# Experts' weights in 2 MB transfers with 16 KB pieces, model columns in another order, and two steps of the norms moved

## The chip, the cores and the metric

The kernel runs on one core of one Trainium2 chip. The metric is the device time of one execution in microseconds; lower is better. Three runs of the kernel before took 1532.81, 1531.54 and 1533.71 us (median 1532.81).

## What is computed

A hybrid encoder of two layers on 256 tokens of 1024 columns, all in float32. Cut to what matters here:

```python
h = layer_norm(x, emb_ln_g, emb_ln_b)
for l in range(2):
    mix = token_mixing(h, ...)                    # four branches, gates, w_branch, w_out
    h = layer_norm(ALPHA * h + mix, ln1_g[l], ln1_b[l])
    ffn = hierarchical_moe(h, ...)                # 32 experts, two per token
    h = layer_norm(ALPHA * h + ffn, ln2_g[l], ln2_b[l])

z = hs @ w_in                                     # 1024 x 8192, split among branches and gates
y_a, y_b, y_c, y_d = ...                          # 2-D window, differential, pooling, dilated
gates = sigmoid(z_gate + b_gate)
merged = sum(gates[n] * (y[n] @ w_branch[n]) for n in range(4))
mix = merged @ w_out

ye = (silu(xb @ w_gate[e]) * (xb @ w_up[e])) @ w_down[e]   # 1024 x 512, 1024 x 512, 512 x 1024
```

An expert has 6 MB of weights, a layer's 32 experts 192 MB (MB is 1024 x 1024 bytes where weights and places are counted; the GB/s of the profile are 10^9 bytes).

## The kernel before

**Stages.** A start (norm of x, `run`, L387), and then per layer `mixing` (L451) and `moe` (L796). `mixing` multiplies the normalised, transposed tokens (kept as a high and a low part, `hth` and `htl`) with column blocks of `w_in`, each block split into a high part by ScalarE (`high`, L232) and a low part by VectorE (`low`, L237), three products for one. There are two forms of product: with tokens in rows (`natural`, L465 in the profile) and with columns in rows (`crosswise`, L484). The four attention and pooling branches come first, then the four gated branch projections in `BRANCH_ORDER` (loop at L756), then `w_out`. `moe` begins with `output_and_route` (L1063: product with `w_out`, norm, router, choice of experts, gather of the first four experts' tokens), then `overflow` (L1324, which runs only where an expert has over 64 tokens), then the loop over 32 experts (L925), and a tail that combines the last expert and starts the next layer.

**The order of the work.** `mixing` is put in order by the framework's scheduler, which places each engine's instructions by its own estimate of when they can run. The start, `output_and_route`, the expert loop and the tail are inside `manual_schedule`, where each engine runs the instructions as written. Each engine is in order, and so is SP, which issues the weights' DMAs: a request that waits for a free place holds those behind it.

**The ring.** All weights pass through places in SBUF of 1 MB: 8 in the pool `rawp` (open throughout), 4 in `rawb` (opened before the third gated branch, L757), 5 in `rawc` (opened by `open_ring`, L128, in the step "ring" of `output_and_route`) and 1 in `rawd` (opened at L871, its load requested at L924, as the expert loop starts). `weight_sources` (L146) gives the order of the transfers, `load_weight` (L181) requests the next one into a new tile of a pool, `take` (L223) hands a source's tiles to the user, and its `free` requests the next transfer into the same pool when a tile has been used. So 17 MB of a layer's experts are requested before the stage, and the 18th as it starts. A transfer of `w_in` is 1 MB in pieces of 2 KB.

**An expert's weights.** Gate and up are each two transfers of 1 MB, in the order gate 0, up 0, gate 1, up 1; each has pieces of 8 KB contiguous in HBM and in SBUF (`f p k`: half, partition, four rows). Down is two transfers of 1 MB (8 KB pieces) and comes behind the next expert's pair. The very last down is two column halves, eight transfers of 256 KB with 1 KB pieces ("halves"). The model columns therefore stand in the order (f p k), in the gathered tokens too (`nat`, `xh`, `xl`: `j=4` in `bk`, L1156).

**The expert loop.** Expert p has twelve steps. Steps 0 to 7 multiply gate and up of one row block each (`products`, L850; L854 in the profile, two matmuls a step), steps 8 to 11 the down-projection of expert p-1 (`down`, L893). After step 3 gate 0 and up 0 are free, after step 7 gate 1 and up 1, after steps 9 and 11 the halves of down. The steps in `STEPS` (copy of the result `evacuate`, `turn`, `silu`, `combine` and so on) and the gather of later experts stand between. The first four steps of expert 0 (`begin`, L856) run before `overflow`.

**Norms.** `turn_rows` (L311, called at L421 for the first norm, outside `manual_schedule`) transposes the norm's scale and shift on TensorE (L317) and copies them with ScalarE (L318). `enter_mixing` (L331) finds the statistics (`norm_stats`, L258; square root on ScalarE, L272), keeps TensorE busy with `FILL[0]` = 28 small matmuls (`keep_busy`, L352; L356 in the profile), and normalises. `finish_h` (L380, called at L537) loads scale and shift as rows (two broadcasts of 512 KB on SP) and applies them to h with four operations on VectorE (L384, L385); its result is needed only where h is added after `w_out`.

**Small tiles.** `t4` has 6 buffers of 4 KB per partition, `t2` 8 of 2 KB. The slots' selection tiles (`gs`, L812) and the overflow's gathered tokens are in `t4`.

Of the kernel before, what the change touches and what calls it, by code (L numbers as in the profile page):

```python
# [29 lines left out]
FILL = (28, 16)  # L30
G = 2
# [75 lines left out]

class Kernel:
# [19 lines left out]
    def open_ring(self):  # L128

        self.close_side()  # L130
        self.side = [self.tc.tile_pool(name=f"rawc{self.layer}", bufs=RAW[2] * 2 // G + 1, side="right", reuse_waits="tile")]
        self.rawc, = (p.__enter__() for p in self.side)
        for _ in range(RAW[2] * 2 // G + 1):
            self.load_weight(self.rawc)

    def close_side(self):
        for p in self.side[::-1]:
            p.__exit__(None, None, None)
        self.side, self.rawc = [], None
# [6 lines left out]
    def weight_sources(self):  # L146
        a = self.a
        for l in range(self.depth):
# [14 lines left out]
            yield l, [(a["const_big"][:, :2048].rearrange("p (k c) -> p k c", k=4), 512)]  # L163
# [9 lines left out]
            for e in range(N_EXP + 1):  # L173
                if e < N_EXP:
                    yield l, [(a[name][l, e].rearrange("(f p k) c -> p f k c", f=2, k=4), 512)
                              for name in ("expert_w_gate", "expert_w_up")], "pair"
                if e:
                    src = a["expert_w_down"][l, e - 1].rearrange("(h p k) d -> p h k d", h=2, k=2)
                    yield l, [(src, D)], "halves" if e == N_EXP else "down"

    def load_weight(self, pool):  # L181

        nc = self.nc
        if self.ahead is None:
            self.ahead, self.part = next(self.sources, None), 0
        if self.ahead is None or (pool in (self.rawb, self.rawc, self.rawd) and self.ahead[0] > self.layer):
            return
        blocks, kind = (*self.ahead[1:], False)[:2]
        if self.part == 0:
            self.loaded.append([[], 1024 // sum(w for _, w in blocks)])  # L190
        qs, q = self.loaded[-1][0], self.part
        if kind:


            parts = 4 if kind == "pair" else 2
            if kind == "pair":
                t = pool.tile([128, 4, 512], F32, tag="raw", name="raw")
                nc.sync.dma_start(t, blocks[q % 2][0][:, q // 2])
            elif kind == "down":
                t = pool.tile([128, 2, 2, 512], F32, tag="raw", name="raw")  # L200
                nc.sync.dma_start(t.rearrange("p k f c -> p k (f c)"), blocks[0][0][:, q])
            else:
                t = pool.tile([128, 4, 2, 256], F32, tag="raw", name="raw")
                src = blocks[0][0].rearrange("p h k (f i c) -> p h k f i c", f=2, i=2)
                for k in range(4):
                    nc.sync.dma_start(t[:, k], src[:, k // 2, k % 2, :, q])
            qs.append((t, pool, True))
            self.part += 1
        else:
            width = sum(w for _, w in blocks)  # L210
            r = 1024 // width
            parts = blocks[0][0].shape[1] // r
            t = pool.tile([128, r * G, width], F32, tag="raw", name="raw")
            o = 0
            for src, w in blocks:
                nc.sync.dma_start(t[:, :, o:o + w], src[:, q * r:(q + G) * r])
                o += w
            qs += [(t[:, i * r:i * r + r], pool, i == G - 1) for i in range(G)]
            self.part += G
        if self.part == parts:  # L220
            self.ahead = None

    def take(self):  # L223
# [3 lines left out]
        def free(i):  # L227
            if qs[i][2]:
                self.load_weight(qs[i][1])
# [158 lines left out]
    def run(self):  # L388
        tc, nc, a = self.tc, self.nc, self.a
        with ExitStack() as ctx:  # L390
            pool = lambda name, bufs, **kw: ctx.enter_context(tc.tile_pool(name=name, bufs=bufs, **kw))
            const = pool("const", 1)
            self.rawp = pool("raw", RAW[0] * 4 // G)
            self.rawb = self.rawc = self.rawd = None
# [1035 lines left out]
```

## Time and profile before

| | us |
|---|---|
| median of three runs | 1532.81 |
| the profiled execution | 1530.08 |
| its span in the trace | 1528.0 |
| TensorE busy | 1467.8 (96%) |
| VectorE busy | 571.0 (37%) |
| ScalarE busy | 468.7 (31%) |
| moved by DMA | 501.16 MB, mean 328 GB/s |

The profile is of one execution: busy time of each engine, the span in 40 slices, and a trace of every instruction with what released it. PE is TensorE, PEld its weight load, DVE VectorE, ACT ScalarE, SP SyncE. The clock is the share of full speed that TensorE was granted. A bracket behind a timeline row tells how long the engine stood idle before it and what ended that. An fp32 matmul leaves two records. Layer 0's expert loop ends near 755 us, layer 1 begins behind it.

### The profile page before, as it was taken

The page shows a single profiled execution, that of the slowest core. Times are in us where ns is not written, and L with a number is a line of the kernel's source. Part 1 is how long each engine was busy: PE and PEld are TensorE (multiplying, and loading weights), DVE is VectorE, ACT ScalarE, POOL GpSimd, SP SyncE. Part 2 cuts the span into 40 slices and gives each one's busy share as a digit, 9 for nine tenths or more (in the row PEclk, how much of TensorE's full clock was granted, in tenths as well). Part 3 has the DMA queues.
Part 4 walks back from the last instruction along what each step waited for, and adds up shares of the span by engine and source line. Part 5 has one row for each costly group of instructions (what it writes and reads, how often), then busy time and mean ns, then how long its engine had stood idle before and what let it go on. Part 6 is the DMA issues. An engine that isn't in the chain of part 4 may idle for free. (4 is left out here: it accounts for less than half of the span.)

```text
span 1528.0 us, 21590 instructions
## 1 busy us (share of the span) xinstructions
PE 1467.8 (96%) x8848; PEld 896.1 (59%) x8848; DVE 571.0 (37%) x1202; ACT 468.7 (31%) x764; POOL 0.2 (0%) x4
## 2 busy tenths in 40 slices
PE   8989999999999999999899999999999999999995
PEld 7777899844444444444378778997444444444432
DVE  5477765721111111111176766665111111111103
ACT  5445555521111111111264555454111111111111
POOL 0000000000000000000000000000000000000000
PEclk9989999999999999999999999999999999999998
DMA  9744485679999999999988336746999999999996
GB/s 334 230 167 138 136 303 195 249 306 419 420 420 419 420 420 419 419 420 421 391 246 308 111 111 214 252 167 254 395 420 420 419 420 420 419 420 420 421 420 217
DMA packets 121658, 501.16 MB, mean 328 GB/s; under 512 B 23050, under 2 KB 35786, under 8 KB 72660
## 3 DMA queue, kind: packets, MB, share of 16 engines
q1 hardware_dynamic: 121248, 499.14, 83.8%
q8 instruction: 72, 1.18, 0.3%
q10 hardware_dynamic: 308, 0.60, 0.1%
q14 instruction: 30, 0.25, 0.0%
HBM read 498.65 MB, written 2.00 MB: 328 GB/s over the span
## 5 line engine op out<-in xcount | busy, mean ns | idle before, releaser
L854 PE MATMUL bank<-raw,xs 128*64 128x512 f32 x2048 | 481.7, 595 | 20.0 <-DMA raw<-in_expert_w_up_dram 19.9
L854 PEld LDWEIGHTS bank<-raw,xs 128*64 128x64 f32 x2048 | 166.3, 137 | 302.2 <-issue 239.5
L896 PE MATMUL bank<-raw,act 128*64 128x512 f32 (+1 forms) x1056 | 261.0, 586 | 0.0
L239 DVE TENSOR_TENSOR wl<-raw,wh 128x1024 fp32r<-128x1024 f32 x159 | 192.6, 1222 | 113.7 <-ACT wh L234 110.0
L876 ACT COPY hid<-bank 128x512 f32<-128x512 f32 x64 | 68.3, 1067 | 457.9 <-PE bank L854 457.9
L234 ACT CAST wh<-raw 128x1024 fp32r<-128x1024 f32 x159 | 165.6, 1050 | 136.6 <-PE mm L484 60.6
L831 DVE COPY xs<-bank 128x256 f32<-128x256 f32 x116 | 43.9, 420 | 421.9 <-PE bank L822 421.9
L484 PE MATMUL mm<-hth,wh 128*128 128x256 f32 x576 | 162.8, 283 | 0.0
L484 PE MATMUL mm<-hth,wl 128*128 128x256 f32 x576 | 162.4, 282 | 0.0
L484 PE MATMUL mm<-htl,wh 128*128 128x256 f32 x576 | 162.2, 282 | 0.0
L896 PEld LDWEIGHTS bank<-raw,act 128*64 128x64 f32 x1056 | 78.4, 136 | 130.8 <-issue 124.6
L908 DVE SCALAR_TENSOR_TENSOR y<-bank,tg,y 128x512 fp32r<-128x512 f32 (+1 forms) x66 | 48.5, 735 | 178.0 <-ACT y L907 178.0
L484 PEld LDWEIGHTS mm<-hth,wh 128*128 128x128 f32 x576 | 109.1, 189 | 2.4 <-issue 2.2
L484 PEld LDWEIGHTS mm<-htl,wh 128*128 128x128 f32 x576 | 109.2, 190 | 1.1 <-issue 0.8
L484 PEld LDWEIGHTS mm<-hth,wl 128*128 128x128 f32 x576 | 109.1, 189 | 1.0 <-issue 0.8
L907 ACT ACTIVATE y<-bank,tg 128x512 fp32r<-128x512 f32 (+1 forms) x66 | 44.5, 674 | 166.2 <-PE bank L896 166.2
L465 PE MATMUL mm<-wh,hth 128*128 128x512 f32 x220 | 72.7, 402 | 1.0 <-ACT hth L300 1.0
L465 PE MATMUL mm<-wl,hth 128*128 128x512 f32 x220 | 71.7, 401 | 0.0
L465 PE MATMUL mm<-wh,htl 128*128 128x512 f32 x220 | 70.2, 398 | 0.0
L822 PEld LDWEIGHTS bank<-g,xh 128*128 128x128 f32 x240 | 36.9, 192 | 50.9 <-issue 50.9
L888 ACT ACTIVATE act<-bank 128x256 f32<-128x256 f32 x64 | 24.6, 385 | 127.7 <-PE bank L882 125.5
L822 PE MATMUL bank<-g,xh 128*128 128x256 f32 x240 | 55.0, 311 | 3.7 <-DVE g L813 3.7
(228 smaller groups left out, 1453.6 us busy)
## 6 DMA issues: line engine op xcount, KB each, us to landing
raw<-in_expert_w_gate_dram SPq DMA_DIRECT2D x128, 1024.0 KB, 19.9
raw<-in_expert_w_up_dram SPq DMA_DIRECT2D x128, 1024.0 KB, 19.9
raw<-in_expert_w_down_dram SPq DMA_DIRECT2D x124, 1024.0 KB, 19.9
raw<-in_w_in_dram SPq DMA_DIRECT2D x56, 1024.0 KB, 7.7
raw<-in_w_in_dram SPq DMA_DIRECT2D x16, 512.0 KB, 11.1
raw<-in_w_branch_dram SPq DMA_DIRECT2D x8, 1024.0 KB, 6.3
raw<-in_w_out_dram SPq DMA_DIRECT2D x8, 1024.0 KB, 8.1
raw<-in_expert_w_down_dram SPq DMA_DIRECT2D x16, 256.0 KB, 13.8
```

Source lines behind the costliest of these rows:

```text
L234: self.nc.scalar.copy(hi, s)
L239: self.nc.vector.tensor_sub(lo, s, raw(hi))
L465: nc.tensor.matmul(ps[T], s[:, kk, T * 128:(T + 1) * 128], m[:, k], stop=kk == 7 and s is stat[1], start=kk == 0 and s is stat[0] and m is wh)
L484: nc.tensor.matmul(ps[j // 2][:, j % 2], m[:, k, j * 128:(j + 1) * 128], s[:, kk], start=j % 2 == 0 and kk == 0 and m is wh and s is hth, ...
L822: nc.tensor.matmul(ps[:, o:o + 256], (xh, xl)[i][:, T, k], gs[e0][:, T], start=i == 0 and T == 0, stop=i == 1 and T == 1)
L831: (nc.scalar.copy if on_scalar else nc.vector.tensor_copy)(xs[e0 + 2 * i][:, :, 2 * j:2 * j + 2], ps[:, 2 * i:2 * i + 2])
L854: nc.tensor.matmul(gu[half[i]], x, w, start=k == 0, stop=k == 7)
L876: nc.scalar.copy(st["h", e].rearrange("q (h k p) -> q h p k", h=2, k=2), gu.rearrange("q (h p k) -> q h p k", h=2, k=2))
L888: nc.scalar.activation(st["a", e], fv[:, :, 0], AF.Silu)
L896: nc.tensor.matmul(ps[half[f], :w.shape[2]], st["a", e][:, k], w[:, f], start=k == 0, stop=k == 3)
L907: nc.scalar.activation(yh, ps, AF.Copy, scale=g)
L908: nc.vector.scalar_tensor_tensor(yl, ps, g, raw(yh), op0=ALU.mult, op1=ALU.subtract)
```

## The change

An expert's gate, up and down become one transfer of 2 MB each, with 16 KB contiguous per partition: gate, up, then the down of the expert before. The model columns stand in the order (p k), eight consecutive rows to a partition, and the inner columns in (p k) with four. Places are of 2 MB (two units): 4 in `rawp`, 2 in `rawb`, 2 in `rawc`. A place is reloaded when all units in it are freed. An odd MB stays: `rawe` (opened with the ring) takes the first half of expert 3's gate, and `load_loose` its second half, in two `t4` tiles of 512 KB (a new step "loose" in `output_and_route`, behind the last transposes of the tokens); later it is reloaded into `rawe` and `rawd` as two transfers of 1 MB with 8 KB pieces. So 18 MB are requested before the stage, and the request at the start of the expert loop is gone. The mixing weights' transfers are what they were, but two share a place; the constants ("alone") have a place for themselves.

`turn_rows` for the first norm moves into the manual schedule ahead of the statistics, `FILL[0]` goes from 28 to 22, `finish_h` moves from the start of `mixing` to before the last gated branch, and `gs` and the overflow's tokens move from `t4` to `t2`.

```diff
-FILL = (28, 16)
+FILL = (22, 16)
...
     def open_ring(self):
         self.close_side()
-        self.side = [self.tc.tile_pool(name=f"rawc{self.layer}", bufs=RAW[2] * 2 // G + 1, side="right", reuse_waits="tile")]
-        self.rawc, = (p.__enter__() for p in self.side)
-        for _ in range(RAW[2] * 2 // G + 1):
+        self.side = [self.tc.tile_pool(name=f"{n}{self.layer}", bufs=b, side="right", reuse_waits="tile")
+                     for n, b in (("rawc", RAW[2] // G), ("rawe", 1))]
+        self.rawc, self.rawe = (p.__enter__() for p in self.side)
+        for _ in range(RAW[2] // G):
             self.load_weight(self.rawc)
+        self.load_first()
...
-                    yield l, [(a[name][l, e].rearrange("(f p k) c -> p f k c", f=2, k=4), 512)
+                    yield l, [(a[name][l, e].rearrange("(p k) c -> p (k c)", k=8), 512)
                               for name in ("expert_w_gate", "expert_w_up")], "pair"
                 if e:
-                    src = a["expert_w_down"][l, e - 1].rearrange("(h p k) d -> p h k d", h=2, k=2)
+                    src = a["expert_w_down"][l, e - 1].rearrange("(p k) d -> p (k d)", k=4)
...
+    def load_odd(self):
+        if self.peek() and self.ahead[0] == self.layer:
+            self.fill([p.tile([128, 2048], F32, tag="raw", name="raw") for p in (self.rawe, self.rawd)], self.load_odd)
+
+    def load_first(self):
+        self.peek()
+        self.odd = self.fill([self.rawe.tile([128, 2048], F32, tag="raw", name="raw")], self.load_odd)
+
+    def load_loose(self):
+        (_, blocks, kind), q = self.ahead, self.part
+        assert kind == "pair" and q % 2
+        ts = [self.t4.tile([128, 2, 512], F32, tag="t4", name="raw") for _ in range(2)]
+        for i, t in enumerate(ts):
+            o = 2048 * (q % 2) + 1024 * i
+            self.nc.sync.dma_start(t.rearrange("p k c -> p (k c)"), blocks[q // 2][0][:, o:o + 1024])
+        self.loaded[-1][0].append((Two(*ts), self.odd))
+        self.odd[0] += 1
+        self.step(4)
...
+            if kind in ("pair", "down"):
...
+                n = 2 if whole is not None and u == q % 2 == 0 else 1
+                o = q % 2 * 2048
+                nc.sync.dma_start(whole if n == 2 else t, src[:, o:o + 2048 * n])
+                qs += [(r(units[u + i]), place) for i in range(n)]
+                place[0] += n
...
         def free(i):
-            if qs[i][2]:
-                self.load_weight(qs[i][1])
+            place = qs[i][1]
+            place[0] -= 1
+            if place[0] == 0:
+                place[1]()
...
             with tc.manual_schedule():
+                self.turn_rows(rows, 0)
                 for T in range(2):
...
             if l == 0:
                 self.router_weights(l)
-            self.finish_h(*(a["ln2_" + n][l - 1] if l else a["emb_ln_" + n] for n in "gb"))
...
+            if n == BRANCH_ORDER[3]:
+                self.finish_h(*(a["ln2_" + n][l - 1] if l else a["emb_ln_" + n] for n in "gb"))
...
-                    gs[e0] = t4.tile([128, 2, batch, CAP], F32R, tag="t4", name="g")
+                    gs[e0] = t2.tile([128, 2, batch, CAP], F32R, tag="t2", name="g")
...
-                nc.scalar.copy(st["h", e].rearrange("q (h k p) -> q h p k", h=2, k=2),
-                               gu.rearrange("q (h p k) -> q h p k", h=2, k=2))
+                nc.scalar.copy(st["h", e].rearrange("q (k p) -> q p k", k=4), gu.rearrange("q (p k) -> q p k", k=4))
...
             with tc.manual_schedule():
-                self.load_weight(self.rawd)
...
-                            i = s // 4 * 2
+                            i = s // 4
                             if p or s >= 4:
-                                products(p, s, tiles[i][:, s % 4], tiles[i + 1][:, s % 4])
+                                products(p, s, tiles[i][:, s % 4], tiles[i + 2][:, s % 4])
                             if s % 4 == 3:
                                 free(i)
-                                free(i + 1)
+                                free(i + 2)
...
-            nc.scalar.copy(xh[:, T, 4 * f:4 * f + 4], nat[T][f])
+            nc.scalar.copy(xh[:, T, :, 64 * f:64 * f + 64], nat[T][f])
...
-                nat[T] = [at().rearrange("q (j p) -> q j p", j=4) for _ in range(2)]
-            i = k % 4 * 32
-            nc.tensor.transpose(nat[T][k // 4][:, :, i:i + 32].rearrange("q j p -> q p j"), piece(T, k), c["ident"])
+                nat[T] = [at().rearrange("q (j p) -> q j p", j=8) for _ in range(2)]
+            i = k % 4 * 16
+            nc.tensor.transpose(nat[T][k // 4][:, :, i:i + 16].rearrange("q j p -> q p j"), piece(T, k), c["ident"])
...
         bks(1)
+        S("loose", self.load_loose)
```

## Rows read from the trace of the kernel before

**Rows 1.** The page: span, engines, DMA share in 40 slices, one of the issue groups

```profile
span 1528.0 us, 21590 instructions
...
PE 1467.8 (96%) x8848; PEld 896.1 (59%) x8848; DVE 571.0 (37%) x1202; ACT 468.7 (31%) x764; POOL 0.2 (0%) x4
...
DMA  9744485679999999999988336746999999999996
...
raw<-in_expert_w_up_dram SPq DMA_DIRECT2D x128, 1024.0 KB, 19.9
```

**Rows 2.** Windows: us, busy PE PEld DVE ACT POOL (x), clock, DMA share, GB/s

```profile
70.00:75.00 5.00, 5.00 (x23) 4.03 (x22) 1.50 (x2) 0.00 (x0) 0.00 (x0) 1.00 1.04 387
86.00:92.00 6.00, 6.00 (x40) 5.34 (x41) 5.92 (x7) 0.00 (x0) 0.00 (x0) 0.54 0.20 37
313.72:317.00 3.28, 2.13 (x18) 2.00 (x18) 0.50 (x2) 0.65 (x2) 0.00 (x0) 1.00 0.69 215
313.70:333.00 19.30, 18.10 (x123) 9.21 (x124) 2.62 (x8) 3.18 (x5) 0.00 (x0) 1.00 0.94 368
400.00:700.00 300.00, 295.75 (x1620) 132.76 (x1616) 51.51 (x123) 45.59 (x64) 0.00 (x0) 1.00 1.01 420
1062.64:1066.00 3.36, 1.97 (x10) 1.97 (x11) 0.53 (x2) 0.04 (x1) 0.00 (x0) 0.74 0.66 222
1062.60:1082.00 19.40, 17.93 (x114) 9.69 (x116) 2.67 (x8) 2.95 (x5) 0.00 (x0) 0.91 0.84 330
```

**Rows 3.** PE's timeline at starts and ends of stages: start, us, instruction, wait before

```profile
314.87 0.50 PE L822 MATMUL bank<-g,xh 128*128 128x256 f32 x2 [1.75 <-DVE g L813]
...
1064.03 0.61 PE L822 MATMUL bank<-g,xh 128*128 128x256 f32 x2 [1.97 <-DVE g L813]
...
1492.95 3.65 PE L854 MATMUL bank<-raw,xs 128*64 128x512 f32 x16 [0.68 <-DMA raw<-in_expert_w_up_dram]
1497.92 3.22 PE L854 MATMUL bank<-raw,xs 128*64 128x512 f32 x13 [1.31 <-DMA raw<-in_expert_w_up_dram]
```

**Rows 4.** DVE's timeline at layer 0's first softmax

```profile
80.55 2.35 DVE L384 TENSOR_TENSOR h<-h,ln 128x1024 f32<-128x1024 f32 x2
82.82 2.35 DVE L385 TENSOR_TENSOR h<-h,ln 128x1024 f32<-128x1024 f32 x2
85.09 0.21 DVE L619 RECIPROCAL m<-m 128x1 f32<-128x1 f32 x2
```

**Rows 5.** PE's timeline behind the first softmax of layer 0 and of layer 1

```profile
85.82 1.97 PE L623 MATMUL at<-cs,p 128*128 128x128 f32 x8 [6.55 <-DVE p L620]
...
834.34 0.66 PE L623 MATMUL at<-cs,p 128*128 128x128 f32 x4 [0.47 <-DVE p L620]
```

**Rows 6.** ACT's timeline at the start

```profile
12.70 0.17 ACT L318 COPY cols<-mm 128x16 f32<-128x16 f32 x1 [9.95 <-PE mm L317]
12.77 0.48 ACT L272 ACTIVATE w<-mv,eps 128x1 f32<-128x1 f32 x2
```

**Rows 7.** DVE's timeline at the start

```profile
10.12 0.27 DVE L273 TENSOR_SCALAR w<-mv 128x1 f32<-128x1 f32 x2
```

**Rows 8.** PE's timeline at the start

```profile
3.67 8.41 PE L356 MATMUL spare<-cs 128*128 128x128 f32 x48 [3.67 <-DMA cs<-in_const_small_dram]
```

**Rows 9.** ACT's timeline at layer 0's first softmax

```profile
80.77 0.71 ACT L618 ACTIVATE p<-p,m 128x512 f32<-128x512 f32 x1
```

**Rows 10.** SP's timeline: first requests of the experts' stages of both layers

```profile
313.72 0.34 SPq L198 DMA_DIRECT2D raw<-in_expert_w_up_dram  x1
...
321.59 0.80 SPq L201 DMA_DIRECT2D raw<-in_expert_w_down_dram  x2
...
1062.64 0.34 SPq L198 DMA_DIRECT2D raw<-in_expert_w_up_dram  x1
...
1072.21 0.80 SPq L201 DMA_DIRECT2D raw<-in_expert_w_down_dram  x2
```

**Rows 11.** The page's costliest groups: DVE's splits of weights in mixing

```profile
L239 DVE TENSOR_TENSOR wl<-raw,wh 128x1024 fp32r<-128x1024 f32 x159 | 192.6, 1222 | 113.7 <-ACT wh L234 110.0
```

More of the change, by code (lines that the diff above doesn't have):

```diff
@@ L179, in weight_sources, with units @@
                     yield l, [(src, D)], "halves" if e == N_EXP else "down"
+    def units(self, pool):
+        t = pool.tile([128, 2, 2048], F32, tag="raw", name="raw")
+        return t.rearrange("p u c -> p (u c)"), [t[:, 0], t[:, 1]]
     def load_weight(self, pool):
-        nc = self.nc
+        if self.peek() and (pool is self.rawp or self.ahead[0] == self.layer):
+            whole, units = self.units(pool)
+            self.fill(units, lambda: self.load_weight(pool), whole)
+    def load_odd(self):
+        if self.peek() and self.ahead[0] == self.layer:
+            self.fill([p.tile([128, 2048], F32, tag="raw", name="raw") for p in (self.rawe, self.rawd)], self.load_odd)
@@ L184, in load_weight, with peek @@
+    def peek(self):
         if self.ahead is None:
             self.ahead, self.part = next(self.sources, None), 0
[L186 to L219, printed above, removed]
@@ L220, in load_weight, with step, fill @@
+        return self.ahead
+    def step(self, parts, n=1):
+        self.part += n
         if self.part == parts:
             self.ahead = None
+    def fill(self, units, reload, whole=None):
+        nc = self.nc
+        place = [0, reload]
+        u = 0
+        while u < len(units) and self.peek():
+            blocks, kind = (*self.ahead[1:], False)[:2]
+            width = 512 if kind == "pair" else sum(w for _, w in blocks)
+            if self.part == 0:
+                self.loaded.append([[], 1024 // width])
+            qs, q, t = self.loaded[-1][0], self.part, units[u]
+            if kind in ("pair", "down"):
+                src, r = blocks[q // 2][0], (lambda x: x.rearrange("p (k c) -> p k c", k=4)) if kind == "pair" else (
+                    lambda x: x.rearrange("p (k f c) -> p k f c", k=2, f=2))
+                n = 2 if whole is not None and u == q % 2 == 0 else 1
[3 more added lines that the diff above has]
+                place[0] += n
+                self.step(4 if kind == "pair" else 2, n)
+                u += n
+                continue
+            if kind == "halves":
+                t = t.rearrange("p (k f c) -> p k f c", k=4, f=2)
+                src = blocks[0][0].rearrange("p (k f i c) -> p k f i c", k=4, f=2, i=2)
+                for k in range(4):
+                    nc.sync.dma_start(t[:, k], src[:, k, :, q])
+                qs.append((t, place))
+                place[0] += 1
+                self.step(2)
+            else:
+                r = 1024 // width
+                parts = blocks[0][0].shape[1] // r
+                t = t.rearrange("p (k w) -> p k w", w=width)
+                o = 0
+                for src, w in blocks:
+                    nc.sync.dma_start(t[:, :, o:o + w], src[:, q * r:(q + G) * r])
+                    o += w
+                qs += [(t[:, i * r:i * r + r], place) for i in range(G)]
+                place[0] += G
+                self.step(parts, G)
+                if kind == "alone":
+                    u += 1
+            u += 1
+        return place
@@ L861, in begin @@
                 for s in range(4):
[L862 removed]
+                    products(0, s, tiles[0][:, s], tiles[2][:, s])
             gu = ahead = None
```

35 lines of the change are left out of this document (19 added, 16 removed).

## The prediction

> **What bounds the kernel now.** I read the page first, then the windows of steady streaming, then SP's timeline where the experts' stage starts, then the places where PE stands still. The page gives a span of 1528.0 us with PE busy for 96% of it and the DMA engines full in both experts' stages and half idle in both mixing stages [rows 1]. So the kernel has two bounds. In mixing it is PE: weights arrive far ahead. In the experts' stage it is the weight stream. It moves 420 GB/s without a gap from 400 to 700 us [rows 2]; PE needs less than that per expert, so it lives on the 17 MiB loaded before the stage until they are used up, and in the last experts of each layer it waits for weights, at the very end 0.68 and 1.31 us before the two halves of the last expert [rows 3]. The layer then ends a fixed chain of work after the last up-projection has landed. Hence an edit of the stream counts only by how much earlier the last pair is in, and an edit of PE's work counts only in mixing, at the start, or behind that landing.
>
> PE has two real gaps outside: 6.55 us at 79.3, where DVE stands between a softmax and its products [rows 4, 5], and the first microseconds.
>
> **The change, part by part.** Sums are against the profiled execution: 1530.08 us, of which 1528.0 is span. The median of the runs shown is 1532.81, 2.7 more; I carry the difference of the sum over to the median. A measurement of this kernel can tell about 0.2%, 3.1 us.
>
> *A. Start.* ACT's square root runs at 12.77, behind the copy of the turned rows, for which ACT waited 9.95 us because PE had filler matmuls queued ahead of the turn [rows 6]. Its operands were there at about 10.25: DVE's step on the same statistics starts at 10.12, with the aggregate before it [rows 7]. With the turn put ahead of the statistics the copy is done early: -2.5 us. Of the 28 fillers 24 take 8.41 us (48 records, two each), 0.35 us one; 22 take 7.7 and keep PE at work to about 12, close to the first transposes of h [rows 8]. Bounds 0 (if the weights, not h, were last) and -2.5.
>
> *B. finish_h away from layer 0's first softmax.* Its four operations hold DVE from 80.55 to 85.09; the reciprocal that leads to PE's 85.82 stands behind them [rows 4, 5]. Without them it waits for the second exponential, which starts at 80.77 and takes 0.71 [rows 9]: it starts at about 81.4, so -3.7. What is late next is PE's own chain, or nothing: in layer 1, where the same four operations fall into a stretch with PE at work, PE fills the same softmax with crosswise products and stands only 0.47 us [rows 5]. Then 6.1 of the 6.55 us go, and what the clock took goes too: at 86 to 92 it was 0.54, after the stop [rows 2], which costs about 3 us at half speed. That end is -9.4 (6.1 + 3.3). The order of this stage is a scheduler's, so I take the middle, -6.
>
> *C. Stream rate.* A piece of 2 KB takes a DMA engine 2048 B / (387/16 GB/s) = 84.7 ns, one of 8 KB 8192 / (420/16) = 312.1 ns [rows 2]. The straight line through both gives 615.3 ns for 16 KB: 426 GB/s. No row has a 16 KB piece, so bounds: nothing (the pieces cost per byte, or are cut), and 436 GB/s, if the two doublings from 387 to 420 (16.5 GB/s each) are followed by a third as large. I take the line, since it is the form in which a fixed cost per piece would show. A MiB takes 2.497 us at 420 and 2.461 at 426. A layer's 192 MiB less the last down-projection and less the 18 MiB loaded before leave 172 to stream; 8 of 9 of them go in 16 KB pieces (the odd place keeps 8 KB): 153 x 0.0352 = -5.4 us per layer, bounds 0 and -14.0.
>
> [...]
>
> *D. Later resume.* The stream stops with the ring full before the stage. Today it resumes at 313.72 in layer 0 and 1062.64 in layer 1 with the extra place, and half a pair later with the next two [rows 10]. After the change a place of 2 MB comes free only when both halves of gate and up are used, which is where the first down-projections are requested today: 321.59 and 1072.21 [rows 10]. That is +7.9 and +9.6. One MiB more is already in: -2.5. The slow start stays, but its sequel, the queue running dry again between the small early requests, goes, since 4 MB are asked for at once. Lost after the resume today: 19.3 x (1 - 368/420) = 2.4 and 19.4 x (1 - 330/420) = 4.2 us, of which 1.6 in the first 3.3 us [rows 2]; so -0.8 and -2.6 go. Net +4.6 and +4.5; I write +4.5 per layer. In the steady stretch the coarser places cost nothing: PE hands back 6 MB per expert, and several requests are always queued (19.9 us from issue to landing, eight transfers of 2.5 us each [rows 1]). That cover ends only if PE falls behind the stream, which it does not.
>
> *E. Tail.* Today the first half of the last pair is multiplied (16 matmuls, 3.65 us by the profile, 3.4 by their spacing) before the second half is in [rows 3]. With up behind gate in two whole transfers no product can start before the last one: +3.4 per layer. Queued behind it on PE are the down-projection of expert 30, its combine and the last expert's chain, all of which DVE and ACT wait for, so all of it shows.
>
> *F. Clock.* The waits of 0.68 and 1.31 [rows 3] become one of about 2 us. Stops of 1.75 us left the clock at full speed, one of 1.97 did not [rows 3]; the stretch behind that one had 0.91 on average over 19.4 us, 1.7 us lost, against 1.00 in layer 0 [rows 2]. In earlier experts the loss eats slack, in the last it shows: 0 to +1.7, I take +0.7 per layer.
>
> [...]
>
> *G. The rest.* finish_h in the last branch: four DVE operations of 1.2 us; there DVE waits for ACT's casts for 113.7 us in 159 operations [rows 11], so they fit. Their two tiles join h's two and the gates of two branches in the six t4 buffers, so the last branch's first gate can wait on ACT for a tile, and PE behind it for a bank; at most one pass of DVE's four operations per layer: bounds 0 and +10, taken +0.3, since DVE is mostly waiting there. Its two loads of 512 KB on SP stand ahead of experts' reloads in a full ring: 0. Mixing reloads only after both halves of a 2 MB place: up to half a place later, covered by the other three, with DMA at 40 to 80% [rows 1]: 0. The two loose loads wait on SP for t4 tiles, with nothing behind them before the resume: 0. Strided split, transposes and hid copy move the same elements: 0, within 0.5 either way. The slots' tiles in t2: 0.
>
> Sum: -2.5 - 6 + 2 x (-5.4 + 4.5 + 3.4 + 0.7) + 0.3 = -1.8. Profiled 1528.3, median **1531.0**.
>
> **The rivals.** *1, slower: no gain of rate.* For it: nothing shows what a piece above 8 KB does, and the busy share at 8 KB already reads 1.01 [rows 2]. Late resume and tail are then unpaid: C is 0, the sum is +9.0, 1541.8. It decides below 425.0 GB/s (4.5 us per layer, no change), and is seen as slower below 423.3.
>
> *2, faster: more rate and the softmax filled.* At 430 GB/s C is -8.9 per layer: 1524.0; with B at -9.4, 1520.6. For it: layer 1 fills that softmax [rows 5], and 387 to 420 shows that larger pieces help. [...] With the full 436 it would be 1513.8; I give that end 0.05 of this rival's chance.
>
> [...]
>
> *3, the change doesn't do what it says in mixing:* the scheduler puts the softmax's casts where they were and PE still stands, or finish_h lands on another critical softmax: B is 0 to -2, 1535 to 1537.
>
> **How the numbers follow.** The forecast, with terms inside their bounds, has 0.45: 0.15 of it faster by over 0.2% (below 1529.7), 0.27 within, 0.03 slower. Rival 1 has 0.17, slower. Rival 2 has 0.30, faster. Rival 3 has 0.08, half within 0.2%, half slower (above 1535.9). Sum: faster 0.45, same 0.31, slower 0.24. The range goes from a little below rival 2 to rival 1, 1519 to 1542, and leaves out about 0.08 below and 0.1 above; the forecast's own is 1526 to 1536.
>
> **What the profile after would show.** A: the square root near 10.3 and the first product near 14.7. B: the stop of 6.55 us gone or about 3 us, the clock at 1.0 behind it. C: a steady window at 425 to 427 GB/s; 420 is rival 1, 430 or more rival 2. D: the first reload after the eighth product pair, then no window below the steady rate. E: 32 products of the last expert after one wait, ending about 2.5 us later relative to the stage's start. F: the clock in the last expert. G: PE without idle time in the last branch. I am wrong if the rate is outside 423 to 430, or if PE waits for weights in the middle of a stage, which would say that the coarse places starve the stream.

## The result and the profile after

The changed kernel took 1539.5 us (median of five runs, 1538.44 to 1543.71) beside 1532.81 (five runs, 1528.42 to 1533.71): ratio 1.0065, 95% interval 1.004 to 1.0089 (the two medians alone give 1.0044). It is slower by 0.65%, where 1531.0 was forecast; the time lies inside the range of 1519 to 1542, on the wrong side of "no change". The ratios below leave out two executions of one kernel, e13, which took 1825.04 and 4205.61 us.

The profiled execution's span is 1536.4 us, 8.4 more than before [rows 1]. Its page:

```profile
span 1536.4 us, 21199 instructions
...
PE 1473.8 (96%) x8836; PEld 891.4 (58%) x8836; DVE 571.1 (37%) x1202; ACT 468.8 (31%) x764; POOL 0.2 (0%) x4
...
DMA  9733585759999999999976236745999999999994
...
raw<-in_expert_w_up_dram SPq DMA_DIRECT2D x64, 2048.0 KB, 30.6
```

128 transfers of 1 MB have become 64 of 2 MB. The steady window, two stretches behind the first softmax and a stretch in which PE was at half clock (columns as in [rows 2]):

```profile
400.00:700.00 300.00, 295.00 (x1608) 131.36 (x1608) 51.34 (x123) 45.08 (x64) 0.00 (x0) 1.00 1.01 426
...
79.50:83.00 3.50, 3.25 (x14) 2.86 (x15) 3.01 (x6) 3.50 (x4) 0.00 (x0) 0.52 0.05 19
...
86.00:92.00 6.00, 5.72 (x49) 5.03 (x48) 5.48 (x13) 2.46 (x5) 0.00 (x0) 1.00 0.70 229
...
309.70:316.10 6.40, 6.33 (x15) 1.80 (x15) 0.47 (x2) 0.00 (x0) 0.00 (x0) 0.57 0.00 0
```

The stream runs at 426 GB/s after 420, as forecast. At 86 to 92 us the clock is 1.00 where it was 0.54; the half clock is not gone but stands at 79.5 to 83.0, behind the shorter stop. At 309.7, in the middle of the first expert, it is 0.57 and no byte moves. PE's timeline there, in layer 0 and in layer 1:

```profile
304.11 1.07 PE L916 MATMUL bank<-raw,xs 128*64 128x512 f32 x2
309.77 6.31 PE L916 MATMUL bank<-raw,xs 128*64 128x512 f32 x14 [4.59 <-SPq L1404]
316.01 0.50 PE L884 MATMUL bank<-g,xh 128*128 128x256 f32 x2
...
1060.39 1.07 PE L916 MATMUL bank<-raw,xs 128*64 128x512 f32 x2
1065.68 5.34 PE L916 MATMUL bank<-raw,xs 128*64 128x512 f32 x14 [4.22 <-SPq L1404]
1070.95 0.51 PE L884 MATMUL bank<-g,xh 128*128 128x256 f32 x2
```

Before, the 16 records of `begin`'s eight matmuls ran in one piece of 3.65 us (309.46 and 1058.41), followed by a stop of 1.75 or 1.97 and the gather [rows 3]. Now one matmul runs, PE stands for over 4 us, and the other seven follow at a clock of 0.57, in layer 1 of 0.68 (1065.6 to 1071.0). What ends the stop is SP at L1404, the head of `overflow`'s loop (L1342 before). From first product to gather it takes 11.90 and 10.56 us after 5.41 and 5.62.

The tail, PE's timeline behind the last landing of each layer:

```profile
746.93 6.65 PE L916 MATMUL bank<-raw,xs 128*64 128x512 f32 x29 [1.48 <-DMA raw<-in_expert_w_up_dram]
...
757.37 3.66 PE L957 MATMUL bank<-raw,act 128*64 128x512 f32 x24
...
1502.17 6.65 PE L916 MATMUL bank<-raw,xs 128*64 128x512 f32 x29 [1.48 <-DMA raw<-in_expert_w_up_dram]
...
1512.63 3.66 PE L957 MATMUL bank<-raw,act 128*64 128x512 f32 x24
```

The same points before were 747.45 and 754.45, 1497.92 and 1504.94. From them the ledger of the 8.4 us (us, after less before, each between two such points):

| stretch | layer 0 | layer 1 |
|---|---|---|
| start, to the first mixing product (17.18 to 14.96) | -2.2 | |
| mixing, to the first expert product | -3.1 | -1.0 |
| first expert product to the gather behind the loop | **+6.5** | **+4.9** |
| gather to the landing of the last pair | -1.7 | -2.7 |
| landing to the last down-projection | +3.4 | +3.4 |
| rest | 0 | +0.7 |

The third line is more than the whole. The experiments are about it first, and then about the tail, the rate and the norms.

### The profile page after: what moved, and what is told of

Same layout as the page of the kernel before. It is cut to its first block, busy times and chain, and to the rows that moved or that the text cites. A ratio compares the mean times of both kernels' runs of the same rounds, so it can differ in the third digit from the quotient of the medians.

```text
span 1536.4 us, 21199 instructions
## 1 busy us (share of the span) xinstructions
PE 1473.8 (96%) x8836; PEld 891.4 (58%) x8836; DVE 571.1 (37%) x1202; ACT 468.8 (31%) x764; POOL 0.2 (0%) x4
## 3 DMA queue, kind: packets, MB, share of 16 engines
q8 instruction: 72, 1.18, 0.3%
## 5 line engine op out<-in xcount | busy, mean ns | idle before, releaser
L916 PE MATMUL bank<-raw,xs 128*64 128x512 f32 x2048 | 493.3, 599 | 27.9 <-DMA raw<-in_expert_w_up_dram 19.1
L957 PE MATMUL bank<-raw,act 128*64 128x512 f32 (+1 forms) x1056 | 265.7, 586 | 0.0
L957 PEld LDWEIGHTS bank<-raw,act 128*64 128x64 f32 x1056 | 82.8, 136 | 125.4 <-issue 116.0
L952 DVE TENSOR_TENSOR act<-act,bank 128x256 f32<-128x256 f32 x64 | 27.0, 422 | 76.5 <-ACT act L949 71.2
```

What stands on the lines that cost most here:

```text
L916: nc.tensor.matmul(gu[half[i]], x, w, start=k == 0, stop=k == 7)
L952: nc.vector.tensor_mul(st["a", e], st["a", e], fv[:, :, 1])
L957: nc.tensor.matmul(ps[half[f], :w.shape[2]], st["a", e][:, k], w[:, f], start=k == 0, stop=k == 3)
```

## The experiments

### Why PE stands at the loop

Two things in the traces could do it. First, SP stops at the loop's head for loads that are still under way. SP's timeline of after, in which the last 6 MB are requested, and its waits at the loop (us in total, times, longest):

```profile
289.48 0.33 SPq L252 DMA_DIRECT2D raw<-in_expert_w_up_dram  x1
289.95 0.34 SPq L252 DMA_DIRECT2D raw<-in_expert_w_down_dram  x1
290.34 0.42 SPq L252 DMA_DIRECT2D raw<-in_expert_w_gate_dram  x1
290.81 1.83 SPq L221 DMA_DIRECT2D raw<-in_expert_w_gate_dram  x2
322.72 0.34 SPq L252 DMA_DIRECT2D raw<-in_expert_w_up_dram  x1
```
```profile
SPq L1404 <- SPq L1404: 4.0, 3, 1.9
```

These waits are instructions of the program. At that line (`tc.For_i` in the source) SP has 16 semaphore instructions per layer (from the view of line L1404: how many, shortest, median and longest in ns, first and last start):

```profile
L1404 SPq EVENT_SEMAPHORE  x32: 17/17/28, 304.6 to 1065.7; - x32
```

The first eight wait for the eight semaphores on which SP's transfers report (in layer 0 they run from 304.57 to 308.86, before from 310.24 to 310.74). Three of them waited for over 0.15 us in layer 0.

DMA's rate in 40 slices of 0.75 us from 300 us, after and before:

```profile
GB/s 415 371 426 437 355 328 284 371 284 60 44 0 22 0 0 0 0 0 0 0 0 0 0 0 0 0 0 0 0 0 0 262 87 350 371 481 415 393 393 502
```
```profile
GB/s 448 426 437 404 470 393 109 0 0 0 0 0 22 0 0 11 0 0 0 109 120 437 393 437 426 448 404 448 404 426 339 251 404 415 426 448 426 339 229 481
```

Before, the ring was full at 305, ahead of the loop at 313; now the last bytes land at 308, with SP already in it from 305. Second, PE's instructions stand in another order, though neither program line was moved: the scheduler put the loop behind the first of the eight matmuls.

```
before  L822 ... L854 MATMUL bank<-raw,xs x8 | L1341 TENSOR_LOAD, L1342 branch, loop | L822 ...
after   L884 ... L916 MATMUL bank<-raw,xs    | L1403 TENSOR_LOAD, L1404 branch, loop | L916 x7, L884 ...
```

**e1_late**: the odd MB is requested behind the loop, so that the loads end before it.

```diff
             self.load_weight(self.rawc)
-        self.load_first()
...
-        S("loose", self.load_loose)
...
             with tc.manual_schedule():
+                self.load_first()
+                self.load_loose()
                 nc.vector.tensor_copy(meta[:, :, :, 1], gates)
```

> The changed kernel with the odd MB (one half of expert 3's gate) and its loose half requested behind the overflow loop, at the start of the expert loop, instead of ahead of it. Theory (the loop's entry waits for every load that is still under way, and the changed kernel's loads end 4 us too late): the loads end near 303 us, PE's wait of 4.6 us in layer 0 and 4.2 us in layer 1 falls to about 2, and the eighth pair of products of expert 0 comes 6.5 us and 3.5 us earlier after its first; about 10 us less than the changed kernel in all. Rival (PE's wait is a slow branch, or the order of the products alone, whatever the loads do): the wait stays above 4 us, and the time is that of the changed kernel within 3 us, or above it since 2 MB less are in.

Ratio 1.0031 (1.002 to 1.0043), span 1531.7: about half of the loss is gone. PE's timeline:

```profile
305.51 3.65 PE L915 MATMUL bank<-raw,xs 128*64 128x512 f32 x16
310.91 0.50 PE L883 MATMUL bank<-g,xh 128*128 128x256 f32 x2 [1.74 <-DVE g L874]
...
1055.57 3.65 PE L915 MATMUL bank<-raw,xs 128*64 128x512 f32 x16
1064.92 0.79 PE L883 MATMUL bank<-g,xh 128*128 128x256 f32 x2 [5.70 <-DMA raw<-in_expert_w_gate_dram]
```

Layer 0 is as before (5.40), and all eight matmuls stand ahead of the loop again. Layer 1 missed the forecast: 9.35, with no ring load left at the loop. There PE's branch out of the loop takes 4.28 us, after 0.39 in layer 0.

**e5_dummy** measures the loop by itself: the kernel before, with two copies of 2 MB added behind the ring's requests, which nothing reads.

```diff
             self.load_weight(self.rawc)
+        for i in range(2):
+            self.nc.sync.dma_start(self.dummy[i], self.a["expert_w_up"][0, i].rearrange("(p k) c -> p (k c)", k=8))
```

> The kernel before with two copies of 2 MB from HBM to HBM requested on SP right behind the ring's last load; nothing reads them. Theory (the overflow loop's entry waits for every load and copy that is under way): in the kernel before the loads end at 305.0 and 1056.4 us, some 5 us ahead of the loop; the copies end 10 to 25 us later, and PE stands until they do, so that the first gather behind the loop comes 7 to 20 us after expert 0's first product instead of 5.4 and 5.6 us, and the execution is longer by that twice. Rival (the loop waits for engines alone): the gather stays within 6 us of the first product, and only the weights' stream is later, 0 to 10 us in all.

One execution: 1541.62, span 1539.6.

```profile
309.77 3.65 PE L857 MATMUL bank<-raw,xs 128*64 128x512 f32 x16
318.73 0.80 PE L825 MATMUL bank<-g,xh 128*128 128x256 f32 x2 [5.30 <-SPq L1345]
...
1063.88 3.65 PE L857 MATMUL bank<-raw,xs 128*64 128x512 f32 x16
1075.79 0.80 PE L825 MATMUL bank<-g,xh 128*128 128x256 f32 x2 [8.26 <-SPq L1345]
```

The copies end near 317.6 and 1074.5, and the gather follows 1.1 and 1.3 us later, 8.96 and 11.91 after the first product. No instruction of the loop or behind it uses those copies: the loop's entry waits for the transfers that SP has under way, needed or not.

**e6_late_act** asks whether e1's loss in layer 1 comes from the late requests on SP: they go to ACT's queue, behind its first gather copy.

```diff
                                 gathered(0, i, ps, i == 2)
+                                if i == 2:
+                                    self.q = nc.scalar
+                                    self.load_first()
+                                    self.load_loose()
+                                    self.q = nc.sync
```

> The kernel of the run with the late odd MB (e1), with these three requests moved on from SP's first place behind the loop to ScalarE's queue, behind its copy of the first gather, so that PE has left the loop before they are made. Theory (PE's branch out of the loop waits for its code behind loads that have just been requested: 4.3 us in layer 1 of e1, 0.4 in layer 0): the branch takes under 1 us in both layers, layer 1's first gather comes 5.4 to 5.8 us after its first product instead of 9.4, and the time is 4 to 6 us below e1. Rival (the slow branch lies with where the code stands, whatever the loads do): 9 us in layer 1 again, and the time of e1.

Ratio 1.0028 (1.0008 to 1.0048), span 1530.5. The branch takes 0.31 us in layer 0 and 3.29 in layer 1, now with no load under way at all; the gather comes 5.32 and 8.29 after the first product. So the slow branch is a third thing, apart from the loads. If it belonged to the place of the code, moving the code would move it.

**e9_pad24, e10_pad44**: e6 with the last pair split (e2 below) and 24 or 44 matmuls of 1x1 at PE's start, which nothing reads.

```diff
+            pd = self.at.tile([128, 512], F32, tag="at", name="pad")
+            for _ in range(24):
+                nc.tensor.matmul(pd[:1, :1], self.eps, self.eps, start=True, stop=True)
```

> e7 with 24 one-by-one matmuls on PE ahead of everything, where PE waits for its first data anyway; all later code of PE stands 96 instructions further on. Theory (whether the branch out of the loop is fast depends on where its code stands): layer 1's branch of 3.5 us, or layer 0's of 0.4, changes by over 2 us in this run or in the one with 44. Rival (layer 1's branch is slow whatever stands before it): 3 to 4 us in layer 1 and under 1 us in layer 0 in both.

> e7 with 44 one-by-one matmuls ahead of everything, 176 instructions. Theory and rival as for the run with 24.

One execution each: 1523.14 and 1528.82, spans 1521.1 and 1526.8. The branch takes 0.31 and 0.37, then 0.31 and 0.28 us; the gather comes 5.38 and 5.38, then 5.38 and 5.27 after the first product, in both layers of both. The same program without the pads (e7) had 3.48 in layer 1. In e10's layer 0 PE then stops for 1.85 us behind the first record of the gather, and goes on at half clock (0.63 us a pair of records instead of 0.40):

```profile
312.42 0.58 PE L894 MATMUL bank<-g,xh 128*128 128x256 f32 x1 [1.85 <-issue]
```

The trace's instruction loads, blocks of 16 KB (72 of them, 1.18 MB, in before, after and e9), show what a slow branch has within it. From the lists of events (us; the two clocks are matched to some 0.2):

```
kernel, layer       branch from..to        load of instructions from
before, 0           313.41..313.72         314.52
after, 0            305.37..308.57         306.08
after, 1            1061.66..1061.95       1063.99
e6_late_act, 1      1058.95..1062.24       1060.12
e9_pad24, 1         1056.77..1057.14       1058.40
```

In the 16 profiled executions there are 12 branches of over 2 us and 20 of under 0.7. Each of the 12 has a load of about 1 us within it, and none of the 20 has. Programs with the same code on PE agree: after and e3 have 3.20 and 0.29, 3.22 and 0.30; e9 and e12, which are one program, are fast in both layers. That a slow branch waits for its code is an inference from these rows; what they show is that it took 2.30 to 5.12 us with a load within it, and 0.28 to 0.65 without.

**e11_after_pad24**: the changed kernel with the 24 pads, to see what the branch had to do with its loss.

> The changed kernel with nothing but the 24 one-by-one matmuls of e9 ahead of everything. Theory (in the changed kernel it is the loads still under way that hold PE at the loop, and the slow branch of 3.2 us in layer 0 lies beside that wait): the branches become fast, and yet the first gather comes 10 to 12 us after expert 0's first product in both layers; the time is that of the changed kernel within 2 us. Rival (the slow branch is the cause in layer 0): layer 0's gather comes about 8 us after the first product, 3 us or more less.

Ratio 1.0064 (1.004 to 1.0088), span 1538.1: nothing won. In layer 0 the branch takes 0.30 us and PE still stands:

```profile
305.83 1.07 PE L919 MATMUL bank<-raw,xs 128*64 128x512 f32 x2
311.17 6.39 PE L919 MATMUL bank<-raw,xs 128*64 128x512 f32 x14 [4.26 <-SPq L1407]
```

Its loss is of the loads and the order, 11.66 us to the gather. In after's layer 0 the slow branch (3.20) ran beside SP's wait and cost little of its own. In layer 1 the forecast missed: the pads made that branch slow, 3.49 us where after has 0.29. It too lies beside SP's wait, whose loads end near 1066.5 there, and the gather comes after 11.62 us instead of 10.56.

**e13_order** parts these two: the loose loads are requested right behind the first half, in the ring's step. The loads are the same ones in the same order, and all eight matmuls stand ahead of the loop.

```diff
         self.load_first()
+        self.load_loose()
...
-        S("loose", self.load_loose)
```

> The changed kernel with the step of the two loose loads moved up to the ring's step: SP issues the same loads in the same order, and on PE the scheduler now leaves all eight matmuls that begin expert 0 ahead of the overflow loop, where the changed kernel has one of them ahead and seven behind it. Theory (the loss at the loop is made of two things that need each other: seven matmuls put behind the loop, and loads that hold it until 308 and 1064 us): with the eight ahead, PE works while the loop waits, and the first gather comes 5.4 to 7 us after the first product in both layers, against 11.9 and 10.6; about 9 us less than the changed kernel. Rival (the loads' wait costs its 4 us whatever stands ahead): the first gather comes 9 to 10 us after the first product, 2 to 4 us less in all.

Ratio 1.0048 (1.0022 to 1.0073), span 1533.4.

```profile
305.94 3.65 PE L917 MATMUL bank<-raw,xs 128*64 128x512 f32 x16
311.65 0.51 PE L885 MATMUL bank<-g,xh 128*128 128x256 f32 x2 [2.06 <-SPq L1404]
...
1056.88 3.65 PE L917 MATMUL bank<-raw,xs 128*64 128x512 f32 x16
1065.37 0.80 PE L885 MATMUL bank<-g,xh 128*128 128x256 f32 x2 [4.83 <-issue]
```

In layer 0 SP's wait, until about 310.8, is still the last to end, but PE has its matmuls to do meanwhile: 5.71 us instead of 11.90. So the same loads cost little when the matmuls stand ahead of the loop. That the late loads are needed as well is read from SP's waits (e11, e5) and not shown by a run of its own: none has the seven matmuls behind the loop and no load under way. Layer 1 has 8.49 by another cause: the loads are in by 1061.2, and a branch of 3.42 us from 1060.74 holds PE, with the gather behind it at half clock (0.63 us a pair of records instead of 0.40). There nothing is won in the end, from the first product to the last pair's landing (442.27 us, after's 441.78), and the span is 3.0 us below after's, not the 9 that were forecast.

### The tail

**e2_split_last**: the last expert's pair as four transfers of 1 MB, in the order of before.

```diff
-                              for name in ("expert_w_gate", "expert_w_up")], "pair"
+                              for name in ("expert_w_gate", "expert_w_up")], "pair" if e < N_EXP - 1 else "split"
...
+            if kind == "split":
+                nc.sync.dma_start(t, blocks[q % 2][0][:, q // 2 * 2048:q // 2 * 2048 + 2048])
...
-                            i = s // 4
+                            i, j2 = (s // 4, s // 4 + 2) if p < N_EXP - 1 else (s // 4 * 2, s // 4 * 2 + 1)
```

> The changed kernel with the last expert's gate and up of each layer in four transfers of 1 MB, gate and up in turn, as the kernel before has them. Theory (the tail costs 3.4 us per layer because no product of the last expert can start before its whole pair is in): half of its products run before the last landing, the time from that landing to the last group of down-projections falls from 10.4 to 7.0 us in both layers, 6.8 us less than the changed kernel in all. Rival (the wait ahead of the products is PE's own pace or the clock's): 0 to 2 us less.

Ratio 1.0064 (1.0044 to 1.0085), span 1540.0. PE's timeline at layer 0's end:

```profile
749.78 7.04 PE L923 MATMUL bank<-raw,xs 128*64 128x512 f32 x32
757.50 1.94 PE L964 MATMUL bank<-raw,act 128*64 128x512 f32 x8 [0.69 <-DMA raw<-in_expert_w_down_dram]
```

PE no longer waits for the last pair, but then for expert 30's down, which is one transfer of 2 MB behind it. From the gather to the last down-projection it takes 447.17 us instead of 448.75, and 447.30 instead of 449.05 in layer 1: -1.6 and -1.75, half of the 3.4. The rest went to the next transfer in the queue. The total does not show it: this execution's mixing took 292.36 and 290.83 us, after's 289.15 and 288.71, with the same instructions.

### The rate

**e3_small**: every transfer of 2 MB is cut into two of 1 MB with pieces of 8 KB; places and order stay.

```diff
-                n = 2 if whole is not None and u == q % 2 == 0 else 1
+                n = 1
```

> The changed kernel with every expert transfer of 2 MB cut into two of 1 MB, with pieces of 8 KB instead of 16 KB, in the same order and into the same places. Theory (the size of the piece sets the rate): steady windows fall from 426 to 420 GB/s, the last pair lands 5.4 us later per layer, and the tail is 3.4 us shorter per layer because the second half of up alone comes after the rest: about 4 us more than the changed kernel. Rival (the size of the transfer, or the fewer requests, sets the rate): steady windows stay at 426, and the time is 7 us less.

Ratio 1.0109 (1.0083 to 1.0135), span 1544.3; the steady window:

```profile
400.00:700.00 300.00, 293.44 (x1594) 124.72 (x1591) 50.10 (x120) 44.68 (x63) 0.00 (x0) 1.00 1.01 420
```

The rate is back at before's 420. From the first request behind the loop to the last pair's landing a layer's stream takes 427.8 us (from 325.90 and 1083.16), 3.6 and 3.3 more than after's, where term C has 5.4; where the rest went was not found. The gain of rate is real, and it is given by the larger transfer or piece; which of the two was not parted. The tail is no shorter: products still waited for the whole pair.

### The norms and the start

**e4_fin_only**: the kernel before with `finish_h` moved. **e8_start_fin**: that and the start's edits.

```diff
-            self.finish_h(*(a["ln2_" + n][l - 1] if l else a["emb_ln_" + n] for n in "gb"))
...
+            if n == BRANCH_ORDER[3]:
+                self.finish_h(*(a["ln2_" + n][l - 1] if l else a["emb_ln_" + n] for n in "gb"))
```

> The kernel before with nothing changed but finish_h, moved to before the last gated branch. Theory (DVE's four operations are what PE waits for at the first softmax): PE's stop of 6.55 us falls to about 2.4, the first product of the experts comes 3 to 6 us earlier in layer 0 and within 1 us in layer 1, and the time is 3 to 5 us below the kernel before. Rival (the last branch gives it back, through its tiles or DVE): within 1 us of the kernel before.

> The kernel before with only the two moves of the norms: the turn of the first norm's rows into the manual order with 22 fillers, and finish_h before the last gated branch. No transfer and no place is changed. Theory (these two steps gain what the traces show, 2.2 us at the start and about 3 in layer 0's mixing; the whole loss is in the transfers' part): 3 to 6 us below the kernel before. Rival (the loss lies in the moves as well): within 2 us of the kernel before or above it.

Ratios 0.9986 (0.997 to 1.0002) and 0.9995 (0.9979 to 1.0012), spans 1530.3 and 1530.6: no gain that can be told, where 3 to 5 and 3 to 6 us were forecast. The profiled executions took 1532.49 and 1532.69 us, 4 us more than the medians of 1528.23 and 1528.44, so their traces may show less than the timed runs gained. The first mixing product of e8 starts at 14.27, 2.9 us earlier (forecast 2.2). Two things took it back in the profiled executions. The new place of the code gave each a slow branch in layer 1 (3.85 and 3.30 us, gather 8.92 and 8.37 after the first product). Layer 0's mixing took 293.59 and 295.36 us, where before had 292.28. In e4 its `crosswise` products are spaced 118 ns almost throughout (4% at 113), before 71% at 113: over some 820 spacings 2.4 us (means of 117.6 and 114.7 ns). Why one execution has the one spacing and the next the other was not found; after and e12, which hold the same move, have 73% and 70% at 113.

### The version that beats both

**e7_late_act_split** joins e6 and e2, **e12_pad24_timed** is e9 again, timed, and **e14_order_split_pad** joins e13, e2 and the pads. The diffs are those above.

> e6 with the last pair in four transfers of 1 MB as in e2. Theory (loop, branch and tail add up): 1.6 us per layer less than e6 as in e2, about 3 us; with e6 as forecast this is 2 to 6 us below the kernel before. Rival (the gains are not additive, the late odd MB comes too late for expert 3): at or above the kernel before.

> The kernel of e9 once more, now timed: late requests behind the loop on ScalarE's queue, the last pair in four transfers, and the 24 one-by-one matmuls. Theory (both branches fast, no load under way at the loop): 4 to 8 us below the kernel before. Rival (e9's single time was a lucky one): within 2 us of the kernel before.

> e13 with the last pair in four transfers and the 24 one-by-one matmuls ahead. Theory: as e12 (4 to 6 us below the kernel before), since the loads' end is hidden under the eight matmuls. Rival (requests behind the loop are better, as the stream then resumes earlier): 2 to 4 us above e12.

| | ratio (95%) | span | branch, layer 0 / 1 | first product to gather |
|---|---|---|---|---|
| e7 | 1.0012 (0.9993 to 1.003) | 1530.2 | 0.39 / 3.48 | 5.39 / 8.55 |
| e12 | **0.9967 (0.9952 to 0.9982)** | 1523.0 | 0.31 / 0.28 | 5.38 / 5.27 |
| e14 | 0.998 (0.9957 to 1.0004) | 1529.1 | 0.31 / 0.65 | 5.32 / 6.00 |

e12 is faster than the kernel before by 0.33% (medians 1524.85 and 1528.63); e7 and e14, also forecast to be below the kernel before, cannot be told from it. What e12 has is late requests off SP, a split last pair, and a fast branch in both layers. PE's timeline at its loop and at layer 0's end:

```profile
304.06 3.65 PE L926 MATMUL bank<-raw,xs 128*64 128x512 f32 x16
309.44 0.50 PE L894 MATMUL bank<-g,xh 128*128 128x256 f32 x2 [1.73 <-DVE g L885]
...
738.03 7.04 PE L926 MATMUL bank<-raw,xs 128*64 128x512 f32 x32
747.31 3.16 PE L967 MATMUL bank<-raw,act 128*64 128x512 f32 x8 [2.25 <-DMA raw<-in_expert_w_down_dram]
```

The loop costs what it did before, and what is left is the wait for the 2 MB down (2.25 us, and the eight records behind it take 3.16 instead of 1.94). Cutting that transfer too was not tried.

## Why the prediction was wrong, step by step

**D, the later resume, is the step that failed.** It priced when SP may request again, and took the entry of `overflow` to be free, since it was free before. The forecast had the resume 12.1 and 13.8 us behind the first expert product; it came at 18.6 and 17.3 (322.72 and 1077.67). The 6.5 and 3.5 us more are the loop (and in layer 1 its slow gathers before, which are gone): the odd MB and the larger last requests end later than the loop begins, its entry waits for them, and the scheduler left seven matmuls behind it, which then run at a clock of 0.57 and 0.68. e5 shows the wait, e13 beside e11 that the order makes it cost. For the same 16 records in layer 0 the stop grew from 1.75 to 4.59 and the work from 3.65 to 7.38. Two sentences of the prediction covered it up: that one MiB more is "already in", and that the loose loads have "nothing behind them before the resume". The loop was behind them, and the prediction named it in no step.

**B** was taken at -6 and gave -3.1 in layer 0's mixing. The stop of 6.55 us became 2.37:

```profile
79.54 1.92 PE L683 MATMUL at<-cs,p 128*128 128x128 f32 x8 [2.37 <-DVE p L680]
```

The stop lost 4.2 us: DVE starts its reciprocal at 78.79, as soon as the exponential ends (78.67, its sum 78.76), and PE has no crosswise products to fill the rest with, as it had in layer 1. One window over the whole of layer 0's mixing, of after:

```profile
14.96:304.11 289.15, 282.06 (x1941) 243.44 (x1941) 199.82 (x386) 158.40 (x271) 0.00 (x0) 0.99 0.63 218
```

Before, PE was busy for 282.12 of 292.28 us. All of the gain is thus idle time, 10.2 less 7.1, since later softmaxes stand about 1 us longer. The clock over 60 to 100 us rose from 0.87 to 0.96, but it is 0.52 right behind the stop (79.5 to 83.0), where the prediction had 1.0, and PE's busy time did not fall; where that went was not found. The step's size was too large by 2.9, from crediting a filled stop and a clock at once.

**A** was right in its number, in part by luck: the square root starts at 9.63 and the first mixing product at 14.96 (forecast 10.3 and 14.7).

```profile
9.63 0.48 ACT L334 ACTIVATE w<-mv,eps 128x1 f32<-128x1 f32 x2 [2.78 <-DVE mv L333]
```

PE's timeline at the start:

```profile
5.67 0.98 PE L379 MATMUL mm<-cs,rows 2*128 2x2 f32 x8 [5.67 <-DMA rows<-in_emb_ln_b_dram]
6.58 7.45 PE L418 MATMUL spare<-cs 128*128 128x128 f32 x44
13.87 1.04 PE L429 MATMUL at<-cs,h 128*128 128x128 f32 x8
```

The fillers now stand behind the turn, which waits for its rows until 5.67, so they run to 14.0 and not to "about 12". They, and not h, are last: ACT has its part of h done at 12.59, and the transposes follow the fillers without a gap. In e2 and e13, with the same start, the fillers run to 15.4 and 15.5 and the first mixing product starts at 16.34 and 16.43, only 0.8 us ahead of before's 17.18.

**C** was right in the rate, from a straight line through two piece sizes: 426 GB/s. From resume to last pair it took 424.2 and 424.5 us; 153 MiB at 2.461 and 19 at 2.497 are 424.0. Undone in e3, it was worth 3.6 and 3.3 us a layer. The upper bound of 436, an extrapolation from the step between 387 and 420, was not reached.

**E** was right: +3.4, the same 10.44 instead of 7.0 us in both layers. **F** was 0 instead of +0.7: stops of 1.48 us in the last experts, where about 2 was forecast, left the clock at 1.00, while the 4.59 at the loop was followed by 0.57 and e12's 2.25 by slow records (eight of them 3.16 us, 1.94 in e2). **G** was near nothing; mixing in layer 1 gained 1.0.

In the prediction's own terms: -2.2 at the start, -3.1 and -1.0 in mixing, twice -0.9 for C and D as forecast, -1.1 by which the resumed streams were shorter than that, twice +3.4 and +0.7 at the end give -1.7, beside the forecast's -1.8. The loop then adds 6.5 and 3.5, and the sum is 8.3 of the 8.4 found. Rival 1 gave nearly this time for a wrong reason: it had the rate at 420. None of the rivals had the loop.

## What to carry to other kernels

In this kernel a dynamic loop in the middle of a stream is a barrier for all that SP has under way (in e5 for two copies that nothing reads, until 317.6 and 1074.5 us): before requests are made larger, later or more, see which of them will still be open at its head, and which instructions of the busy engine stand behind it. A gain of rate is worth only what the coarser request leaves of it at both ends of the stream; here 5.4 us a layer were won in the middle, and 4.5 lost at the start and 3.4 at the end by forecast alone. When two kernels differ by code, compare their branches too, since an edit far away moved one from 0.29 to 3.49 us (e11, layer 1).

## What was not expected of the hardware

- The loop's entry waited for two copies that nothing used, until 317.6 and 1074.5 us (e5). This is of the program, which waits for SP's semaphores there, and not of the chip.
- A branch out of a loop that does not run took 0.28 to 0.65 us or 2.30 to 5.12, by the place of the code; small matmuls at the start made it fast in both layers (e9, e10, e12), or moved it from layer 0 to layer 1 (e11).
- The same mixing instructions differ by 3 to 4 us from kernel to kernel (layer 0's take 289.15 us in after, 292.36 in e2, 292.81 in e3): crosswise products are spaced 113 or 118 ns, and stretches at half clock come or not (10.2 us of them in layer 0's mixing before, 3.4 after, 10.2 in e2 and e3). The cause stays open, as does why the scheduler moved seven matmuls.
